# Late up products of three feed-forward layers as [feature, token], with the high and low activations side by side

## The chip, the cores and the metric

The kernel runs on one core of one Trainium2 chip. The metric is the device time of one execution in microseconds. TensorE (PE in the rows) multiplies: a stationary 128 x 128 operand is loaded (PEld), and a moving operand of up to 512 columns streams past it into PSUM. VectorE (DVE), ScalarE (ACT) and GpSimd (POOL) do the rest, and SyncE (SP) issues the DMAs of the weights. Each engine works through its own queue in order and waits for semaphores of the others.

## The reference, cut to what matters

Two transformer blocks run one after the other over 256 tokens of width 1024, each with two layers. Only the feed-forward parts and the norms behind them matter here:

```python
def first_block(x, ...):                      # RMS norms, x + ...
    for l in range(DEPTH):                    # DEPTH = 2
        ...                                   # two attentions, gates, w_out
        h2 = rms_norm(x, mlp_norm_g[l])
        x = x + jnp.square(jax.nn.relu(h2 @ w_up[l])) @ w_down[l]        # 1024 -> 4096 -> 1024

def _swiglu(x, w1, w3, w2):                   # 1024 -> 2816 -> 1024
    return (jax.nn.silu(x @ w1) * (x @ w3)) @ w2

def second_block(x, mem, ...):
    a = DEEPNORM_ALPHA
    for l in range(DEPTH):
        x = _layer_norm(a * x + 0.5 * _swiglu(x, ffn1_w1[l], ffn1_w3[l], ffn1_w2[l]), ...)
        mix = _token_mixing(x, w_in[l], ...)  # four branches, ends with @ w_o
        x = _layer_norm(a * x + mix, ...)
        x = _layer_norm(a * x + _cross_attention(x, mem, ...), ...)
        x = _layer_norm(a * x + 0.5 * _swiglu(x, ffn2_w1[l], ffn2_w3[l], ffn2_w2[l]), ...)
```

All of it is in float32.

## The kernel before, in words

**Numbers.** A float32 operand is held as two tiles, the high part (a rounded copy in the type fp32r, made by ScalarE) and the low part (what the rounding left, subtracted by VectorE). A product of two operands is three products per 128-deep K tile: high x high, high x low weights, low x high weights, all added in PSUM. `mm_a` (L423) issues them with a 128-token half of the activations as the stationary operand and up to 512 columns of weights moving, so that the result is [token, feature]. The 256 tokens are two halves, m = 0 and 1; the residual rows of the halves are the tiles x0 and x1.

**Weights.** They arrive in the order of use as units of 512 KB (128 partitions x 1024 numbers, here two K tiles x 512 columns). SyncE issues their DMAs into the pool `raw` of 7 buffers, ScalarE casts the high part (L325) and VectorE subtracts the low part (L318); these two are called a conversion here. Conversions run about five units ahead of the use (`LOOK`), and not more than 11 (`WIDE`) or 9 (`NARROW`) units past the oldest one that is held. High and low parts, the activations `xt` of a stage and others share the pool `b4` of 27 buffers.

**A feed-forward stage** is `ffn` (L695). The stage's activations stand in `xt`, eight K tiles x 256 tokens, high and low apart. `up` (L702) makes the products of one chunk of 512 features (in swiglu the last chunk has 256) for both halves, per matrix; `act_relu2` or `act_swiglu` makes h of them, still [token, feature]. The down product needs features on partitions, so `trans` (L729) transposes h on TensorE, four 128 x 128 blocks per half and chunk (L419), and splits the result into high and low (L570, L571, or L573, L574 with a scale). `dn` (L750) is the down product: six 512-column products per half, output half of D and unit. The first chunks (two in w_up, one in each swiglu matrix) go through `gemm_first` (L492), which begins with half 0 while half 1 is still being normalized.

**The end of a stage** is `leave` (L536), used by `ffn` and by `gemm_out` (the projections w_out, w_o and that of the cross attention). It runs the last three units of a down or output product for half 0, then for half 1, with the chains `update` (L639) of the halves beside them. A chain is, on VectorE: for each half of D, x updated from PSUM (L646 or L648) and its statistics (L652); then the aggregate (L657), x less its mean times the gain (L670), the reciprocal root in eight small steps (L589 to L596), and x times that plus the bias (L672). Then `transposed` (L681) turns x0, later x1, on TensorE into the next stage's `xt` and splits it (L570, L571). The last layer norm of the program writes the output instead.

**What sets the order.** A list scheduler orders the instructions of every engine when the program is built, by dependencies, priorities and its own estimate of durations. The chains have a high priority (`hasten`, L370); conversions have none. On the chip the order of each engine's queue is fixed.

## Time and profile before

| | us |
|---|---|
| median of 3 runs | 2226.20 |
| lowest and highest | 2226.19, 2227.69 |
| the profiled execution | 2228.81 |
| its span in the profile | 2227.0 |
| TensorE busy | 2187.6 (98%) |
| VectorE busy | 1520.3 (68%) |
| ScalarE busy | 1078.1 (48%) |
| GpSimd busy | 118.7 (5%) |

The mean granted clock of TensorE in the profiled execution is 0.997 of full. In the rows, a line such as L413 is a line of the kernel before; `mm` (L413) issues every product and `tr` (L419) every transpose, so shapes and tile names tell the work apart. The mean of one matmul that a group prints is longer than its share of the busy time, since matmuls overlap in the pipeline; busy time divided by the count is what one adds to the stream. Of a row with brackets the bracket is the idle time before it and what ended that.

### The profile page before, as it was taken

The numbers are of one execution on the slowest core, as the hardware profiler recorded it, in microseconds if no ns is written. First come the engines' busy times: TensorE is split into PE (matmuls) and PEld (weight loads), VectorE is DVE, ScalarE is ACT, GpSimd is POOL, SyncE is SP. The second block draws the span as 40 slices with busy tenths as digits, with TensorE's granted clock in tenths as the row PEclk, the third lists the DMA queues.
The fourth block names the chain that finished last, engine by engine and source line by source line (L and its number), as shares of the span: only waits on it lengthen the run. The fifth ranks groups of instructions, "written<-read, shape, count | busy, mean of one in ns | idle before, by whom it ended". The sixth has DMA issues, their size and how long they took to land. (4 is left out here: it accounts for less than half of the span.)

```text
span 2227.0 us, 30615 instructions
## 1 busy us (share of the span) xinstructions
PE 2187.6 (98%) x11454; PEld 1852.9 (83%) x11454; DVE 1520.3 (68%) x2456; ACT 1078.1 (48%) x1681; POOL 118.7 (5%) x191
## 2 busy tenths in 40 slices
PE   7999999999999999999999999999999999999998
PEld 6878888878888888889888888888888988897886
DVE  7677457768545555888878765575578887777555
ACT  5664444583434444466654444444345665444442
POOL 2000001000000000013000000000000310000000
PEclk9999999999999999999999999999999999999999
DMA  7355465445555555454556455555645554754561
GB/s 272 117 168 193 167 221 168 152 144 185 172 207 176 184 208 203 162 181 151 171 182 206 157 185 208 208 167 192 229 153 184 170 152 152 235 181 151 181 244 48
DMA packets 114709, 399.91 MB, mean 180 GB/s; under 512 B 13056, under 2 KB 13728, under 8 KB 114560
## 3 DMA queue, kind: packets, MB, share of 16 engines
q1 hardware_dynamic: 107712, 374.30, 49.4%
q0 software_dynamic: 6848, 23.66, 3.2%
q8 instruction: 90, 1.47, 0.3%
q14 instruction: 59, 0.48, 0.1%
HBM read 396.85 MB, written 1.05 MB: 179 GB/s over the span
## 5 line engine op out<-in xcount | busy, mean ns | idle before, releaser
L413 PE MATMUL ps<-b,b 128*128 128x512 f32 (+7 forms) x10412 | 2090.1, 363 | 5.4 <-DVE b L571 2.5
L413 PEld LDWEIGHTS ps<-b,b 128*128 128x128 f32 (+2 forms) x10412 | 1736.8, 188 | 316.3 <-issue 11.3
L318 DVE TENSOR_TENSOR b<-raw,b 128x1024 fp32r<-128x1024 f32 (+3 forms) x738 | 844.6, 1181 | 50.5 <-PE ps L413 28.9
L325 ACT CAST b<-raw 128x1024 fp32r<-128x1024 f32 (+3 forms) x738 | 717.3, 1019 | 197.5 <-PE ps L413 138.8
L570 ACT CAST b<-ps 128x512 fp32r<-128x512 f32 (+2 forms) x188 | 100.8, 571 | 394.6 <-PE ps L419 313.7
L571 DVE TENSOR_TENSOR b<-ps,b 128x512 fp32r<-128x512 f32 (+2 forms) x188 | 118.7, 663 | 194.8 <-ACT b L570 194.4
L574 DVE SCALAR_TENSOR_TENSOR b<-ps,b 128x512 fp32r<-128x512 f32 (+1 forms) x64 | 39.1, 653 | 257.5 <-ACT b L573 257.5
L573 ACT ACTIVATE b<-ps 128x512 fp32r<-128x512 f32 (+1 forms) x64 | 33.1, 569 | 342.8 <-PE ps L419 342.8
L419 PE MATMUL ps<-cst,b 128*128 128x128 f32 (+1 forms) x810 | 106.6, 274 | 13.3 <-DVE b L667 11.6
L419 PEld LDWEIGHTS ps<-cst,b 128*128 128x128 f32 (+1 forms) x810 | 93.8, 140 | 25.3 <-DVE b L667 11.8
L601 POOL DMA_DIRECT2D b<-in_rows_dram x55 | 29.7, 543 | 1363.5 <-PE ps L413 743.6
L1544 ACT ACTIVATE b<-b,sm 128x128 f32<-128x128 f32 (+1 forms) x128 | 56.6, 447 | 7.9 <-DVE sm L819 7.8
L786 DVE TENSOR_TENSOR b<-b,ps 128x512 f32<-128x512 f32 (+1 forms) x48 | 30.8, 642 | 38.6 <-PE ps L413 37.3
L879 DVE TENSOR_TENSOR b<-ps,b 128x512 f32<-128x512 f32 x32 | 22.1, 689 | 27.1 <-PE ps L413 27.0
L881 ACT ACTIVATE b<-b 128x512 f32<-128x512 f32 x32 | 20.0, 630 | 41.8 <-DVE b L879 41.8
L652 DVE BATCH_NORM_STATS2 sm<-x 128x6 f32<-128x512 f32 x48 | 32.8, 688 | 3.9 <-DMA x<-in_x_dram 3.6
L1564 DVE TENSOR_TENSOR b<-b,sm 128x512 f32<-128x512 f32 x48 | 34.2, 740 | 0.3
L775 ACT ACTIVATE b<-ps 128x512 f32<-128x512 f32 x32 | 19.3, 603 | 28.4 <-PE ps L413 28.4
L784 ACT ACTIVATE b<-ps 128x512 f32<-128x512 f32 (+1 forms) x48 | 27.0, 562 | 12.0 <-issue 7.3
L785 DVE SCALAR_TENSOR_TENSOR b<-b,ps 128x512 f32<-128x512 f32 (+1 forms) x48 | 30.7, 639 | 0.0
L776 DVE SCALAR_TENSOR_TENSOR b<-ps,b 128x512 f32<-128x512 f32 x32 | 21.8, 688 | 12.6 <-ACT b L775 12.6
L419 PE MATMUL ps<-cst,x 128*128 128x128 f32 x128 | 19.5, 286 | 10.5 <-DVE x L672 10.4
(170 smaller groups left out, 753.5 us busy)
## 6 DMA issues: line engine op xcount, KB each, us to landing
raw<-in_ffn_w_dram SPq DMA_DIRECT2D x248, 512.0 KB, 5.7
raw<-in_w_in_dram SPq DMA_DIRECT2D x184, 512.0 KB, 4.6
raw<-in_w_up_dram SPq DMA_DIRECT2D x64, 512.0 KB, 5.0
raw<-in_w_down_dram SPq DMA_DIRECT2D x64, 512.0 KB, 4.9
b<-in_rows_dram POOLq DMA_DIRECT2D x19, 512.0 KB, 7.0
raw<-in_w_out_dram SPq DMA_DIRECT2D x16, 512.0 KB, 4.4
raw<-in_ffn_w_dram SPq DMA_DIRECT2D x32, 256.0 KB, 2.9
raw<-in_w_o_dram SPq DMA_DIRECT2D x16, 512.0 KB, 5.7
```

What stands on the lines that cost most here:

```text
L318: self.nc.vector.tensor_sub(lo[:, :n], r[:, :n], hi[:, :n].bitcast(F32))
L325: self.nc.scalar.copy(hi[:, :n], r[:, :n])
L413: i = self.nc.tensor.matmul(out, lhsT, rhs, start=start, stop=stop, skip_group_check=True)
L419: i = self.nc.tensor.transpose(out, in_, self.ident[:k, :k])
L570: nc.scalar.copy(hi, src)
L571: nc.vector.tensor_sub(lo, src, hi.bitcast(F32))
L573: nc.scalar.activation(hi, src, AF.Copy, scale=scale)
L574: nc.vector.scalar_tensor_tensor(lo, src, scale, hi.bitcast(F32), op0=ALU.mult, op1=ALU.subtract)
L652: nc.vector.bn_stats(st[:, 6 * i:6 * i + 6], x[:, c])
L786: nc.vector.tensor_mul(h[:, :w], r[:, :w], pss[1])
L1544: nc.scalar.activation(p[:, i], p[:, i], AF.Exp, scale=-1.0, bias=nm[:, at + i:at + i + 1], accum_out=den[:, at + i:at + i + 1])
L1564: e.tensor_mul(p, p, rinv[:, at:at + n].unsqueeze(2).broadcast_to((P, n, w)))
```

## The change

From a stage's third chunk on (w_up) or the second (each swiglu matrix), the up products take 256 features at a time. The weights are now the stationary operand and the activations move: high and low activations stand side by side in one constant tile (`StageXT`, 8 K tiles x 2 x 256), so the high weights see 512 columns (high and low activations at once) and the low weights 256. The result is [feature, token], with the products of the low activations in a PSUM half of their own; ScalarE copies that half out and VectorE adds the other to it. `late_relu2` and `late_swiglu` work on the sum, and the split writes the operand of the down product directly, without transposes, into the pool `b2`. A unit of these chunks holds four K tiles x 256 columns. The pool `b4` loses four buffers, those that the stage's `xt` used. `leave` takes the last three units as before.

```diff
+FIRST_UPS = {"w_up": 2, "ffn1_w1_2": 1, "ffn1_w3_2": 1, "ffn2_w1_2": 1, "ffn2_w3_2": 1}
+def _ups(name, n):
+    m = 512 * FIRST_UPS[name]
+    return _even(m) + [[(i, i + 256)] for i in range(m, n, 256)]
...
-    "w_up": (D, _even(FF1)),
+    "w_up": (D, _ups("w_up", FF1)),
...
+def _deep(name, c):
+    return 4 if c >= FIRST_UPS.get(name, 99) else 2
...
     def open(self, ctx):
...
-        for tag, bufs in (("raw", RAW), ("b4", B4 - RAW), ("b2", B2), ("b1", B1), ("h", 8), ("sm", 24)):
+        for tag, bufs in (("raw", RAW), ("b4", B4 - RAW - 4), ("b2", B2), ("b1", B1), ("h", 8), ("sm", 24)):
...
+        self.xt_tile = self.const.tile([P, 8, 2, S], F32R, name="xt")
...
     def leave(self, name, l, us, product, acc, a, kind):
...
-        self.xt = self.new_xt()
+        self.xt = StageXT(self.xt_tile)
...
-    def ffn(self, l, ups, down, act, scale, a, kind):
+    def ffn(self, l, ups, down, act, late_act, scale, a, kind):
...
-        def up(c, between):
-            pss = [[], []]
-            for i, name in enumerate(ups):
-                nu, cw = self.dims(name, c)
-                ps = [self.ps(), self.ps()]
-                for u in range(nu):
-                    unit = self.get(name, l, c, u)
-                    for m in range(2):
-                        self.mm_a(ps[m][:, :cw], xt, m, unit, cw, 2 * u, 2, u == 0, u == nu - 1)
...
+        def up(c, between=None):
+            both = []
+            for i, name in enumerate(ups):
+                ps = [self.ps() for _ in range(2)]
+                for u in range(2):
+                    unit = self.get(name, l, c, u)
+                    for f in range(2):
+                        for k in range(4):
+                            o = k * 256 + f * P
+                            first, last = u == 0 and k == 0, u == 1 and k == 3
+                            self.mm(ps[f], unit[0][:, o:o + P], xt.both(4 * u + k), first, False)
+                            self.mm(ps[f][:, :S], unit[1][:, o:o + P], xt.get(4 * u + k)[0], False, last)
+                        if u == 1:
+                            if f == 0:
+                                both.append(self.t("b2", [P, 2, S]))
+                            s = both[-1][:, f]
+                            nc.scalar.copy(s, ps[f][:, S:])
+                            nc.vector.tensor_add(s, ps[f][:, :S], s)
...
+            h = late_act(both)
+            t = XT(self, 2, "b2")
+            hi, lo = t.pair(0)
+            self.split(hi, lo, h, scale)
+            ht[2 * ahead + c - ahead] = t, 0
...
+        up_first(range(ahead))
+        todo = deque(range(us - 3))
         if ahead == 2:
-            trans(seq[0])
-            dn([0, 1])
-        for i in range(ahead, n):
...
+            trans(0)
+            dn(todo.popleft())
+            dn(todo.popleft())
+        n = len(WEIGHTS[ups[0]][1])
+        for c in range(ahead, n):
+            if c == n - 1:
+                kind = kind()
+            up(c, (lambda: trans(ahead - 1)) if c == ahead else None)
+            if c != n - 2:
+                dn(todo.popleft())
+        while todo:
+            dn(todo.popleft())
+        self.leave(down, l, range(us - 3, us), product, acc, a, kind)
...
+    def late_relu2(self, both):
+        h = self.t("b2", [P, 2, S])
+        self.nc.vector.scalar_tensor_tensor(h, both[0], 0.0, both[0], op0=ALU.max, op1=ALU.mult)
+        return h
+    def late_swiglu(self, both):
+        nc, (a, b) = self.nc, both
+        r = self.t("b2", [P, 2, S])
+        nc.scalar.activation(r, a, AF.Tanh, scale=0.5)
+        nc.vector.scalar_tensor_tensor(r, r, 1.0, a, op0=ALU.add, op1=ALU.mult)
+        nc.vector.tensor_mul(r, r, b)
+        return r
...
+class StageXT:
...
+    def get(self, k, m=None):
+        c = slice(0, S) if m is None else slice(m * P, m * P + P)
+        return self.t[:, k, 0, c], self.t[:, k, 1, c]
+    def both(self, k):
+        return self.t[:, k].rearrange("p h t -> p (h t)")
```

The line numbers move: L318, L413, L419 are L335, L430, L436 in the changed kernel; the chain's L648, L657, L670, L672 are L666, L675, L688, L690, and the root's L589 to L596 are L607 to L614. The new copy and addition are L763 and L764.

In the order of the built program, TensorE in the late chunks of w_up, layer 0 of block 1. A row names the result in PSUM, then the moving and the stationary operand. Before: products of a chunk (`b_489`, `b_490` are weights, high and low, `b_373`, `b_374` activations), then transposes of the chunk ahead, then the chunk's next unit:

```order
L413 MATMUL ps_2357<-b_489_2284,b_373_1746 128x512
L413 MATMUL ps_2357<-b_490_2285,b_373_1746 128x512
L413 MATMUL ps_2357<-b_489_2284,b_374_1747 128x512 x2
L419 MATMUL ps_2396<-cst,b_486_2277 128x128 x4
L419 MATMUL ps_2403<-cst,b_488_2281 128x128 x4
L413 MATMUL ps_2356<-b_492_2302,b_375_1748 128x512
L413 MATMUL ps_2356<-b_493_2303,b_375_1748 128x512
```

After, in such a chunk, where `b_514` and `b_519` are high, `b_515` and `b_520` low weight tiles:

```order
L430 MATMUL ps_2568<-xt,b_514_2456 128x512
L430 MATMUL ps_2568<-xt,b_515_2457 128x256
L430 MATMUL ps_2568<-xt,b_514_2456 128x512
L430 MATMUL ps_2568<-xt,b_515_2457 128x256
L430 MATMUL ps_2567<-xt,b_519_2476 128x512
L430 MATMUL ps_2567<-xt,b_520_2477 128x256
```

The eight transposes between the products are gone, and products of 512 and 256 columns alternate.

VectorE at the end of ffn1 in layer 0 of block 2, before: the chain of x0 from the aggregate to its last step (x0 and x1 are the halves' rows, sm small tiles, ps PSUM):

```order
L657 BN_AGGR sm_1656_7881<-sm_1655_7880 128x2
L670 SCALAR_TENSOR_TENSOR x0_82<-x0_82,sm_1656_7881,b4_1591_7604 128x512 x2
L589 TENSOR_SCALAR sm_1663_7917<-sm_1656_7881 128x1
L590 TENSOR_SCALAR sm_1664_7918<-sm_1663_7917 128x1
L584 SCALAR_TENSOR_TENSOR sm_1665_7919<-sm_1664_7918,sm_1663_7917 128x1
L592 SCALAR_TENSOR_TENSOR sm_1665_7919<-sm_1665_7919 128x1
L593 SCALAR_TENSOR_TENSOR sm_1664_7918<-sm_1665_7919,sm_1664_7918 128x1
L584 SCALAR_TENSOR_TENSOR sm_1665_7919<-sm_1664_7918,sm_1663_7917 128x1
L595 SCALAR_TENSOR_TENSOR sm_1664_7918<-sm_1665_7919,sm_1664_7918 128x1
L596 TENSOR_SCALAR sm_1664_7918<-sm_1664_7918 128x1
L672 SCALAR_TENSOR_TENSOR x0_82<-x0_82,sm_1664_7918,b4_1592_7606 128x512 x2
L648 SCALAR_TENSOR_TENSOR x1_83<-x1_83,ps_1441_6843 128x512
```

After, the same place from the aggregate on; x0's last step (L690) follows six rows below the last one shown, with one more conversion among them:

```order
L675 BN_AGGR sm_1665_8174<-sm_1664_8173 128x2
L688 SCALAR_TENSOR_TENSOR x0_83<-x0_83,sm_1665_8174,b4_1623_7981 128x512 x2
L607 TENSOR_SCALAR sm_1672_8210<-sm_1665_8174 128x1
L335 TENSOR_TENSOR b4_1676_8232<-raw_1654_8135,b4_1675_8231 128x1024
L608 TENSOR_SCALAR sm_1673_8211<-sm_1672_8210 128x1
L335 TENSOR_TENSOR b4_1688_8293<-raw_1659_8151,b4_1687_8292 128x1024
L602 SCALAR_TENSOR_TENSOR sm_1674_8212<-sm_1673_8211,sm_1672_8210 128x1
L335 TENSOR_TENSOR b4_1695_8318<-raw_1660_8153,b4_1694_8317 128x1024
L610 SCALAR_TENSOR_TENSOR sm_1674_8212<-sm_1674_8212 128x1
L335 TENSOR_TENSOR b4_1698_8332<-raw_1663_8165,b4_1697_8331 128x1024
L666 SCALAR_TENSOR_TENSOR x1_84<-x1_84,ps_1439_6988 128x512
L611 SCALAR_TENSOR_TENSOR sm_1673_8211<-sm_1674_8212,sm_1673_8211 128x1
```

Conversions and an update of x1 moved between the small steps of x0's chain.

TensorE at the same place, before, where `ps_1446` gathers the last down product of half 1 and the transposes are those of x0:

```order
L413 MATMUL ps_1446_6863<-b4_1632_7800,b4_1636_7819 128x512 x2
L413 MATMUL ps_1446_6863<-b4_1643_7838,b4_1635_7818 128x512
L419 MATMUL ps_1671_7972<-cst_81,x0_82 128x128 x4
L413 MATMUL ps_1446_6863<-b4_1644_7839,b4_1635_7818 128x512
L419 MATMUL ps_1672_7979<-cst_81,x0_82 128x128 x4
L413 MATMUL ps_1446_6863<-b4_1643_7838,b4_1635_7818 128x512
L413 MATMUL ps_1446_6863<-b4_1644_7839,b4_1635_7818 128x512
L413 MATMUL ps_1446_6863<-b4_1643_7838,b4_1636_7819 128x512 x2
```

After, with `ps_1439` in the same part:

```order
L430 MATMUL ps_1439_6988<-b4_1652_8131,b2_1644_8091 128x512
L430 MATMUL ps_1439_6988<-b4_1653_8132,b2_1644_8091 128x512
L430 MATMUL ps_1439_6988<-b4_1652_8131,b2_1645_8092 128x512 x2
L436 MATMUL ps_1680_8265<-cst_82,x0_83 128x128 x4
L436 MATMUL ps_1681_8272<-cst_82,x0_83 128x128 x4
L430 MATMUL ps_1690_8298<-b4_1655_8143,xt_79 128x440
```

The last five products of half 1 stand ahead of x0's transposes, and the next product behind these is the first of the next stage.

## Rows read from the trace of the kernel before

**Rows 1.** Page, part 1: busy us (share of the span) and instructions.

```profile
PE 2187.6 (98%) x11454; PEld 1852.9 (83%) x11454; DVE 1520.3 (68%) x2456; ACT 1078.1 (48%) x1681; POOL 118.7 (5%) x191
```

**Rows 2.** Waits on PE: line, waited for: us in total, times, longest.

```profile
PE ps L419 <- DVE x L672: 10.4, 9, 2.5
```

**Rows 3.** Groups by shape on PE: count, then busy us, mean ns, idle before.

```profile
L413 PE MATMUL ps<-b,b 128*128 128x512 f32 x7344 | 1708.2, 392 | 3.7 <-ACT b L570 1.1 <-DVE b L571 1.0 <-DVE b L318 1.0
L413 PE MATMUL ps<-b,b 128*128 128x256 f32 x2296 | 291.5, 286 | 1.5 <-DVE b L571 1.5
L419 PE MATMUL ps<-cst,b 128*128 128x128 f32 x776 | 102.4, 275 | 13.3 <-DVE b L667 11.6 <-ACT b L570 0.8 <-DVE b L629 0.5
```

**Rows 4.** Groups by shape on PE from 740 to 900 us, in ffn1.

```profile
L413 PE MATMUL ps<-b,b 128*128 128x512 f32 x634 | 145.5, 390 | 0.0
L413 PE MATMUL ps<-b,b 128*128 128x256 f32 x96 | 11.9, 284 | 0.0
```

**Rows 5.** Timeline of PE, 300 to 332 us: start, us, instruction [wait].

```profile
318.52 1.03 PE L419 MATMUL ps<-cst,b 128*128 128x128 f32 x8
319.31 12.95 PE L413 MATMUL ps<-b,b 128*128 128x512 f32 x56
```

**Rows 6.** Windows, ffn1: PE, PEld, DVE, ACT, POOL busy; PEclk, DMA share, GB/s.

```profile
735.00:905.00 170.00, 170.00 (x819) 143.26 (x818) 92.46 (x103) 71.89 (x87) 1.06 (x2) 1.00 0.54 198
```

**Rows 7.** Groups by shape: an addition from PSUM and a copy out of it.

```profile
L1673 DVE TENSOR_TENSOR b<-ps,b 64x256 f32<-64x256 f32 x48 | 18.7, 418 | 6.8 <-ACT b L1672 6.2
L1672 ACT COPY b<-ps 64x256 f32<-64x256 f32 x48 | 16.7, 366 | 3.3 <-PE ps L413 1.2 <-DVE b L1673 0.8
```

**Rows 8.** Timeline, 895 to 935 us: end of ffn1 in layer 0, into mixing.

```profile
903.61 0.68 DVE L648 SCALAR_TENSOR_TENSOR x<-x,ps 128x512 f32<-128x512 f32 x1
...
907.84 0.14 DVE L589 TENSOR_SCALAR sm<-sm 128x1 f32<-128x1 f32 x1
908.02 0.15 DVE L590 TENSOR_SCALAR sm<-sm 128x1 int32<-128x1 int32 x1
...
910.56 0.66 PE L419 MATMUL ps<-cst,x 128*128 128x128 f32 x4 [0.58 <-DVE x L672]
...
918.53 0.15 DVE L589 TENSOR_SCALAR sm<-sm 128x1 f32<-128x1 f32 x1
918.59 1.22 DVE L318 TENSOR_TENSOR b<-raw,b 128x1024 fp32r<-128x1024 f32 x1
919.72 0.15 DVE L590 TENSOR_SCALAR sm<-sm 128x1 int32<-128x1 int32 x1
...
924.63 1.32 PE L419 MATMUL ps<-cst,x 128*128 128x128 f32 x8 [1.60 <-DVE x L672]
```

**Rows 9.** Timeline: ends of w_o, xattn, ffn2 in layer 0, two of layer 1.

```profile
1220.38 0.63 PE L419 MATMUL ps<-cst,x 128*128 128x128 f32 x4 [0.24 <-DVE x L672]
...
1222.87 1.28 DVE L652 BATCH_NORM_STATS2 sm<-x 128x6 f32<-128x512 f32 x2
...
1279.80 1.38 PE L419 MATMUL ps<-cst,x 128*128 128x128 f32 x8 [2.53 <-DVE x L672]
...
1467.94 1.29 PE L419 MATMUL ps<-cst,x 128*128 128x128 f32 x8
...
1671.48 1.32 PE L419 MATMUL ps<-cst,x 128*128 128x128 f32 x8 [1.60 <-DVE x L672]
...
2028.22 1.79 PE L419 MATMUL ps<-cst,x 128*128 128x128 f32 x8 [2.52 <-DVE x L672]
```

**Rows 10.** Windows behind four waits of TensorE; PEclk is the third number from the end.

```profile
1281.00:1285.00 4.00, 4.00 (x12) 3.09 (x12) 3.95 (x8) 3.47 (x5) 0.00 (x0) 0.59 0.00 0
1672.00:1677.00 5.00, 4.98 (x19) 4.07 (x18) 3.57 (x9) 1.79 (x3) 0.00 (x0) 0.66 0.60 206
2028.00:2032.00 4.00, 3.78 (x14) 3.06 (x15) 3.61 (x8) 2.54 (x4) 0.00 (x0) 0.57 0.00 0
925.00:930.00 5.00, 4.98 (x27) 4.16 (x26) 4.77 (x11) 2.42 (x4) 0.00 (x0) 1.00 0.65 209
```

More of the change, by code (lines that the diff above doesn't have):

```diff
@@ L117, in _units @@
         for c, ch in enumerate(chunks):
-            for u in range((k // P + 1) // 2):
-                nk = min(2, k // P - 2 * u)
+            d = _deep(name, c)
+            for u in range((k // P + d - 1) // d):
+                nk = min(d, k // P - d * u)
                 out[(l, c, u)] = (off, nk, _width(ch))
@@ L134, in _pack @@
         at = 0
+        first = _deep(name, c) * u * P
         for a, b in chunks[c]:
-            blk = w[l, 2 * u * P:(2 * u + nk) * P, a:b].reshape(nk, P, b - a)
+            blk = w[l, first:first + nk * P, a:b].reshape(nk, P, b - a)
             dst[:, :, at:at + b - a] = blk.transpose(1, 0, 2)
@@ L481, in dims @@
         k, chunks = WEIGHTS[name]
-        return (k // P + 1) // 2, _width(chunks[c])
+        d = _deep(name, c)
+        return (k // P + d - 1) // d, _width(chunks[c])
     def nk(self, name, u):
@@ L692, in into_xt @@
             yield
-    def ffn(self, l, ups, down, act, scale, a, kind):
-        hid = WEIGHTS[down][0]
-        n = (hid + 511) // 512
+    def ffn(self, l, ups, down, act, late_act, scale, a, kind):
+        nc = self.nc
+        us = WEIGHTS[down][0] // 256
         xt = self.xt
+        ahead = FIRST_UPS[ups[0]]
         acc = [[None, None], [None, None]]
         hs, ht = {}, {}
-        def up(c, between):
-            pss = [[], []]
-            for i, name in enumerate(ups):
-                nu, cw = self.dims(name, c)
-                ps = [self.ps(), self.ps()]
-                for u in range(nu):
-                    unit = self.get(name, l, c, u)
-                    for m in range(2):
-                        self.mm_a(ps[m][:, :cw], xt, m, unit, cw, 2 * u, 2, u == 0, u == nu - 1)
-                    if i == 0 and u == nu // 2 - 1:
-                        between()
-                for m in range(2):
-                    pss[m].append(ps[m][:, :cw])
-            for m in range(2):
-                hs[c, m] = act(pss[m], cw)
         def up_first(cs):
@@ L729, in trans @@
         def trans(c):
-            ht[c] = self.new_xt(4)
+            t = self.new_xt(4)
             for m in range(2):
-                h, w = hs.pop((c, m))
+                h, _ = hs.pop((c, m))
                 ps = self.ps()
-                k = w // P
-                for i in range(k):
+                for i in range(4):
                     self.tr(ps[:, i * P:i * P + P], h[:, i * P:i * P + P])
-                hi, lo = ht[c].block(0, m, k)
-                self.split(hi, lo, ps[:, :w].rearrange("p (k t) -> p k t", k=k), scale)
-        nus = [(min(512, hid - 512 * c) + 255) // 256 for c in range(n)]
-        seq = [c for c in range(n) if nus[c] == 2]
-        seq[1:1] = [c for c in range(n) if nus[c] == 1]
-        first_u, last_u = 0, 2 * seq[-1] + 1
+                hi, lo = t.block(0, m)
+                self.split(hi, lo, ps.rearrange("p (k t) -> p k t", k=4), scale)
+            ht[2 * c] = t, 0
+            ht[2 * c + 1] = t, 2
+        def up(c, between=None):
[16 more added lines that the diff above has]
+                            nc.vector.tensor_add(s, ps[f][:, :S], s)
+                    if i == 0 and u == 0 and between is not None:
+                        between()
+            h = late_act(both)
[3 more added lines that the diff above has]
+            ht[2 * ahead + c - ahead] = t, 0
         def product(m, cc, u, unit):
@@ L747, in product, with dn @@
                 acc[m][cc] = self.ps()
[L748 to L769 removed]
+            t, k = ht[u]
+            self.mm_a(acc[m][cc], t, m, unit, 512, k, 2, u == 0, u == us - 1)
+        def dn(u):
+            for cc in range(2):
+                unit = self.get(down, l, cc, u)
+                for m in range(2):
+                    product(m, cc, u, unit)
+        up_first(range(ahead))
+        todo = deque(range(us - 3))
+        if ahead == 2:
+            trans(0)
[4 more added lines that the diff above has]
+            if c == n - 1:
+                kind = kind()
+            up(c, (lambda: trans(ahead - 1)) if c == ahead else None)
[4 more added lines that the diff above has]
+        self.leave(down, l, range(us - 3, us), product, acc, a, kind)
     def act_relu2(self, pss, w):
@@ L1029, in swiglu @@
         self.nu = WIDE
[L1030 removed]
+        self.ffn(l, [f"{which}_w1_2", f"{which}_w3_2"], f"{which}_w2_2", self.act_swiglu, self.late_swiglu, 0.25, ALPHA, kind)
     def block2(self, l):
@@ L1456, in pair, with __init__, block @@
         return hi[:, k:k + 2], lo[:, k:k + 2]
+class StageXT:
+    def __init__(self, t):
+        self.t = t
+    def get(self, k, m=None):
[3 more added lines that the diff above has]
+        return self.t[:, k].rearrange("p h t -> p (h t)")
+    def block(self, k, m, n=4):
+        c = slice(m * P, m * P + P)
+        return self.t[:, k:k + n, 0, c], self.t[:, k:k + n, 1, c]
 class Group:
```

28 lines of the change are left out of this document (6 added, 22 removed).

## The prediction

> **What bounds the kernel now.** I read the busy table of the page first. TensorE is busy 98% of the span, VectorE 68%, ScalarE 48% [rows 1]; with one core and a TensorE that hardly rests, the time is the sum of TensorE's instructions plus its waits plus what a lowered clock costs. So the change has two accounts: what it does to the number and length of TensorE's instructions, and what it does to TensorE's few waits. The second view is the table of waits on TensorE: the entry that belongs to stages the change touches is 10.4 us in 9 waits for L672, the last step of a layer norm [rows 2]. These are the ends of the stages of block 2: the normed half x0 or x1 must be finished on VectorE before TensorE can transpose it. Nothing in the feed-forward stage itself holds TensorE up: between 735 and 905 us it is busy 170.00 of 170 us, with VectorE at 92.46 and ScalarE at 71.89 [rows 6]. So what the change gains must come from TensorE's own instructions in the feed-forward stages, and what it may lose must come at the layer norms, where VectorE is on the path.
>
> **Part 1: instructions of TensorE.** Per 512 late features and K tile, six products of 512 columns become four of 512 and four of 256: the same 3072 columns, two more instructions. Over the program (3072 late features in two layers of w_up, 2304 in eight swiglu matrices, whose last 256 features were already 256 columns wide) that takes away 576 products of 512 columns and adds 1152 of 256. The groups by shape give 1708.2/7344 = 232.6 ns for 512 columns and 291.5/2296 = 127.0 ns for 256 [rows 3] (busy over count; the mean printed beside it counts overlap twice). So -576 x 0.2326 = -134.0 us and +1152 x 0.1270 = +146.3 us: **+12.3 us**. In the stretch 740 to 900 the same division gives 229.5 and 124.0 ns [rows 4], and so +10.7 us.
>
> The transposes of the activations go: 24 late chunk halves of 512 columns in w_up (96 transposes) and 144 in swiglu, 240 in all. By group 102.4/776 = 132 ns each [rows 3]: **-31.7 us**. The other end is the distance of starts: eight of them at 318.52, the next product at 319.31, so 99 ns each [rows 5], which gives -23.8 us. I take the group's figure, since it is what a long stream is worth: net **-19.4 us**; the ends are -13.1 (99 ns, stretch prices) and -21.0 (132 ns, stretch prices).
>
> The surplus of 12.3 us is a fixed part of each instruction, some 21 ns beyond half of a 512-column product here. The Trainium skill, in TensorE: Matmul & The Clock Gate, section Back-to-back issue gap, gives an isolated gap of N/2.4 + 2.5 ns for N columns at the full clock; by that the exchange would cost only about 1.4 us (an estimate by that page) and the sum would be 11 us lower. The stream here shows 232.6 ns where the rule gives 215.8, so the rows decide.
>
> **Part 2: VectorE and ScalarE in the feed-forward stages.** Each chunk of 256 features and matrix now ends with two ScalarE copies out of PSUM and two VectorE additions, 128x256. The nearest rows are a copy and an addition from PSUM of 64x256: 366 and 418 ns [rows 7]. A swiglu has 9 chunks x 2 matrices x 2 = 36 of each: at most 15 us more on VectorE and 13 on ScalarE, before the splits that are saved. 92.46 + 15 and 71.89 + 13 of 170 us leave a third of VectorE free, and TensorE has a group of down products between one chunk's evacuation and the need for its result. I price this at nothing; if the cover fails it is rival 4. The weight DMAs of the last chunks become fewer and larger, and SP issues them several units ahead of their use: nothing. The one shared tile of stage activations can be written only when the stage before has read it; its readers stand whole groups of down products earlier: nothing.
>
> **Part 3: where VectorE's conversions stand.** This is the part that the diff does not tell. The scheduler placed VectorE's weight conversions (L318, 1.2 us each) anew. I counted in the order those that stand in x0's chain, from x0's second update to its last step, at the seven layer-norm ends that follow a matrix product and lead into another stage: end of ffn1 1 before, 6 now (both layers); of w_o 2 and 8 (both); of xattn 1 and 7 (both); of ffn2 in layer 0 1 and 6. That is **39 more**. At five of these ends (all but xattn, which had it) x1's second update and its statistics also come into x0's chain. The pieces of order above show the first end.
>
> What one costs is seen in x1's chain at this same end before. Without a conversion between them L589 and L590 start at 907.84 and 908.02, 0.18 us apart; with one they start at 918.53 and 919.72, 1.19 us apart [rows 8]. So an inserted conversion of 1.22 us lengthens the chain by **1.01 us**, a little less than its duration. x1's update (0.68 [rows 8]) and statistics (1.28/2 = 0.64 [rows 9]) by the same share add 1.1 us. Longer chains: ffn1 5 x 1.01 + 1.1 = 6.2; w_o 6 x 1.01 + 1.1 = 7.2; xattn 6 x 1.01 = 6.1; ffn2 5 x 1.01 + 1.1 = 6.2.
>
> What covers it? Before, TensorE already waits for x0 at three of the four kinds of end: 0.58 at ffn1, 0.24 at w_o, 2.53 at xattn; at ffn2 it does not wait [rows 8, 9]. So there is no slack, and the chain's growth goes into the wait, less the products that are now ahead of the transposes instead of behind them: five at ffn1 and w_o (5 x 0.23 = 1.2 us), and about as much at ffn2 with its unknown slack. Growth of the waits: 5.0 twice, 6.0 twice, 6.1 twice, 5.0 once: **+39.2 us**.
>
> On the other side x1's chain loses its conversions (four to six of them), and TensorE has its 24 first products of the next stage and more in front of x1's transposes as before. Of the 10.4 us waited for L672 [rows 2], x0's are 2 x (0.58 + 0.24 + 2.53) = 6.7, if the second layer is as the first; the other 3.7, such as the 1.60 at 924.63 [rows 8], may go: **-3.7 us**. The ends of block 1 (rms) keep their order.
>
> **Part 4: the clock after a wait.** After the 2.53 us wait the granted clock from 1281 to 1285 is 0.59 of full, that is largely the 1.2 GHz level, and TensorE was idle for part of the six us ahead of it; 4 x 0.41 = 1.6 us are lost. After a wait of 1.60 us it is 0.66 from 1672 to 1677 (1.7 us), after one of 2.52 us 0.57 from 2028 to 2032 (1.7 us). After the 1.60 us wait at 924 it stays at 1.00 [rows 8 to 10]. Three of four waits of this length cost about 1.7 us, 5.0 in all. With seven longer waits, at the same three in four: 7 x 0.75 x 1.7 = 8.9, so **+3.9 us**.
>
> **Sum.** -19.4 + 39.2 - 3.7 + 3.9 = **+20.0 us**. Against the profiled execution of 2228.8 that is 2248.8; the median of the runs stands 2.6 us below the profiled one, so I forecast 2226.2 + 20.0 = **2246.2 us**, slower by 0.9%. A difference of about 0.2% (4.5 us) is what a measurement of this kernel can tell from none.
>
> **Rivals.**
> 1. *Only TensorE's account counts.* If VectorE stood so far ahead of TensorE at the stage ends that its conversions were done before x0's second product ends, the chain would not lengthen and 2226.2 - 19.4 = 2206.8 would result: faster. For it: VectorE is busy only 68%. Against it: its queue is in order, the conversions stand behind x0's second update, which needs TensorE's last product of x0, and before x0's chain TensorE already waits. It decides if the x0 waits stay below 2.8 us each (19.4/7). Chance 0.06.
> 2. *The clock.* If the low level lasted as long as the wait before it, seven waits of 5.6, 6.2, 8.6 (twice each) and 5.0, 45.8 us in all, would cost half of it, 22.9 us, where I put 8.9: 2260. For it: three waits of 1.6 to 2.5 us were each followed by 1.6 to 1.7 lost. Against it: at 924 nothing followed. The Trainium skill (the same page, section HAM oscillation — how this bites in real kernels) has idle stretches of TensorE followed by a throttled one; by that the loss would come after each of the seven, and the trace agrees at three of four. Chance 0.08.
> 3. *The two accounts cancel.* If the conversions cost about half (0.5 us) because they fill gaps of the chain's dependent small steps, +39.2 becomes about +20 and the time stays at 2226. Against it: the 1.19 against 0.18 in rows 8. Chance 0.04.
> 4. *The evacuation holds TensorE.* If at each of the 60 late chunks (24 in w_up, 36 in swiglu) TensorE waited 0.5 us for copy and addition before its PSUM is free, 30 us would come on top: 2276. Against it: the free third of VectorE and the down products in between. Chance 0.04.
>
> That the change doesn't do what it says is excluded by the order of the built program: the transposes are gone and the 256-column products are there.
>
> **How the numbers follow.** The forecast has 0.78. Its own ends: with the larger gain (-21.0), conversions at 0.85 us (39 x 0.16 = 6 less) and no change of the clock, +8: 2234; with the smaller gain (-13.1), conversions at 1.16 and x1's waits kept, +36: 2262, which takes in rival 2. Range 2234 to 2262; outside are rivals 1, 3 and 4 with 0.14. Faster 0.07, same 0.04, slower 0.89.
>
> **What the changed profile would show.** Part 1: some 11790 matmuls, 256-column products at 124 to 127 ns and TensorE still without a wait in the feed-forward stages; a wait for the new L763 or L764 there would mean rival 4. Part 3: the waits for x0's last step (L690) at the seven ends of 5 to 9 us, 46 us in all, with conversions (L335) between the small steps in the timeline of VectorE. Waits of 1 to 3 us there would make the prediction wrong towards rival 1. Part 4: clock at 0.5 to 0.7 for 3 to 5 us behind most of these waits; if for as long as the wait, rival 2.

## The result and the profile after

The changed kernel takes **2265.45 us** (median of 4 runs, 2264.35 to 2265.97) against 2226.94 us for the kernel before in the same job (4 runs): ratio 1.0167, 95% interval 1.0155 to 1.0179, or 38.5 us slower. The forecast was 20.0 us slower, with a range up to 2262. The direction and the mechanisms were right; two terms of the sum, the gain of TensorE's own instructions and the price of the clock, were mis-sized by 17 us together. The profiled execution took 2265.97 us, its span is 2264.2, 37.2 more than before.

The page's busy table (answers to [rows 1]):

```profile
PE 2189.5 (97%) x11790; PEld 1865.9 (82%) x11790; DVE 1623.8 (72%) x2620; ACT 1154.2 (51%) x1825; POOL 116.0 (5%) x191
```

336 more matmuls (576 products more, 240 transposes fewer), and TensorE's busy time is nearly what it was: what its own instructions gained, a lower clock took back, as is read below. In the feed-forward stage nothing holds it, as before [rows 6]; the window of ffn1, same columns:

```profile
730.00:900.00 170.00, 170.00 (x882) 144.74 (x881) 110.19 (x135) 85.32 (x118) 1.06 (x2) 1.00 0.58 187
```

170.00 of 170 us busy; VectorE rose from 92.46 to 110.19 and ScalarE from 71.89 to 85.32 (the prediction had 107 and 85). So the copies and additions are hidden, and rival 4 is out.

The time is lost at the stage ends. Waits of TensorE (answers to [rows 2]), then the timeline of its x0 transposes at four of the seven ends (ffn1, w_o, xattn, ffn2 of layer 0; answers to [rows 8, 9]):

```profile
PE ps L436 <- DVE x L690: 45.2, 7, 8.6
```

```profile
909.36 1.94 PE L436 MATMUL ps<-cst,x 128*128 128x128 f32 x8 [4.80 <-DVE x L690]
...
1225.19 1.94 PE L436 MATMUL ps<-cst,x 128*128 128x128 f32 x8 [6.82 <-DVE x L690]
...
1292.25 1.94 PE L436 MATMUL ps<-cst,x 128*128 128x128 f32 x8 [8.60 <-DVE x L690]
...
1486.68 1.94 PE L436 MATMUL ps<-cst,x 128*128 128x128 f32 x8 [4.80 <-DVE x L690]
```

Seven waits, 45.2 us, where the prediction put 45.8; all are x0's, x1's are gone. That is 34.8 us more than the 10.4 of before. All idle time of TensorE, span less busy time, rose from 39.4 to 74.7 us, so by 35.3: these waits are nearly all of it. Eight transposes now take 1.94 us instead of the 1.38 that eight take behind a short wait at the full clock (e5_fill below): the clock is down. VectorE at the first of these ends shows why x0 is late (timeline, 900 to 909 us):

```profile
900.57 0.15 DVE L607 TENSOR_SCALAR sm<-sm 128x1 f32<-128x1 f32 x1
900.63 1.22 DVE L335 TENSOR_TENSOR b<-raw,b 128x1024 fp32r<-128x1024 f32 x1
901.77 0.15 DVE L608 TENSOR_SCALAR sm<-sm 128x1 int32<-128x1 int32 x1
901.83 1.22 DVE L335 TENSOR_TENSOR b<-raw,b 128x1024 fp32r<-128x1024 f32 x1
902.96 0.22 DVE L602 SCALAR_TENSOR_TENSOR sm<-sm,sm 128x1 f32<-128x1 f32 x1
903.09 1.22 DVE L335 TENSOR_TENSOR b<-raw,b 128x1024 fp32r<-128x1024 f32 x1
...
905.43 0.68 DVE L666 SCALAR_TENSOR_TENSOR x<-x,ps 128x512 f32<-128x512 f32 x1
...
908.46 1.42 DVE L690 SCALAR_TENSOR_TENSOR x<-x,sm,b 128x512 f32<-128x512 f32 x2
```

From the first small step at 900.57 to x0's last step at 908.46 are 7.9 us; before it was 907.84 to 909.75, 1.9 us. Each conversion that stands between two small steps pushes the next one by 1.2 us. These conversions are of 1024 columns: they belong to the second group of weights of the next stage, whose products begin only behind x0's transposes and the first 24 products; the last of the 880-column ones, which come first, started at 888.28.

The clock behind the seven waits (windows, columns as in [rows 10]):

```profile
909.00:912.00 3.00, 2.64 (x10) 2.40 (x11) 2.93 (x7) 1.17 (x2) 0.00 (x0) 0.52 0.32 130
1225.00:1230.00 5.00, 4.81 (x23) 4.84 (x24) 4.90 (x11) 1.17 (x2) 0.00 (x0) 0.50 0.59 210
1292.00:1298.00 6.00, 5.75 (x17) 4.71 (x18) 5.76 (x15) 2.22 (x3) 0.00 (x0) 0.50 0.35 139
1486.00:1493.00 7.00, 6.32 (x19) 5.18 (x20) 6.65 (x18) 2.21 (x3) 0.00 (x0) 0.51 0.37 147
1681.00:1687.00 6.00, 5.82 (x19) 5.27 (x20) 5.72 (x16) 2.22 (x3) 0.00 (x0) 0.50 0.15 60
1999.00:2005.00 6.00, 5.62 (x27) 5.65 (x28) 5.76 (x15) 1.18 (x2) 0.00 (x0) 0.52 0.47 172
2066.00:2070.00 4.00, 3.31 (x12) 2.87 (x13) 3.93 (x8) 1.17 (x2) 0.00 (x0) 0.54 0.67 246
```

Behind each of the seven, TensorE runs at the 1.2 GHz level for 3 to 7 us. Length times what is missing to 1, as the prediction counted it: 1.4 + 2.5 + 3.0 + 3.4 + 3.0 + 2.9 + 1.8 = 18.0 us, against 5.0 before. That count is too high: it takes in idle time, up to 0.7 us in a window, and it takes every instruction to be twice as long at half the clock, which the eight transposes above are not (1.94 us against 1.38). Two runs below keep the clock up and allow a direct comparison. From x0's transposes to the first product behind x1's, the same instructions take **13.3 us** less in e5_fill than here, summed over the seven ends. TensorE is busy for 4.1 us less in e7_before_behind, where no wait is followed by a low clock, than in the kernel before (2183.5 against 2187.6). So the clock costs about 9 us more than before, not 13.

The span's 37.2 us are then 35.3 of waits and 9.2 of clock, less some **7 us** that TensorE's own instructions got shorter. That rest can be compared with the stream itself. TensorE in ffn1 after (timeline; a group of `ps<-xt,b` holds 512- and 256-column products in turn, and is printed by the shape of its first):

```profile
753.78 5.64 PE L430 MATMUL ps<-b,b 128*128 128x512 f32 x24
759.26 11.45 PE L430 MATMUL ps<-xt,b 128*128 128x512 f32 x64
770.55 5.67 PE L430 MATMUL ps<-b,b 128*128 128x512 f32 x24
```

64 late up products take 770.55 - 759.26 = 11.29 us, 352.8 ns a pair; 24 down products 5.48 us, 228.3 ns each. 1536 pairs are 541.9 us; the 2112 products of 512 columns that they replace, at 228.3, and the 384 of 256 at the 124.0 of [rows 4] are 529.8. That is +12.1 us, as forecast (+12.3). The transposes were worth 240 x 99 ns = 23.8 us [rows 5], not the 31.7 I took: net -11.7. The span leaves 7, so the pieces overstate the gain by 4 to 5 us. Some 1.6 of them come with the constant tile alone (TensorE busy 2183.5 us in e7_before_behind, 2185.1 in e8_xt_behind, which adds the tile and the smaller pool); the other 3 are not placed.

### The profile page after: what moved, and what is told of

Read it like the earlier page. It is cut to its first block, busy times and chain, and to the rows that moved or that the text cites. A ratio compares the mean times of both kernels' runs of the same rounds, so it can differ in the third digit from the quotient of the medians.

```text
span 2264.2 us, 31445 instructions
## 1 busy us (share of the span) xinstructions
PE 2189.5 (97%) x11790; PEld 1865.9 (82%) x11790; DVE 1623.8 (72%) x2620; ACT 1154.2 (51%) x1825; POOL 116.0 (5%) x191
## 4 chain that ended last, share of the span: by engine, by line
PE 85%; DVE 7%; issue 5%; ACT 2%; DMA 1%; POOL 0%; SPq 0%; DVEq 0%; ACTq 0%; POOLq 0%
PE ps L430 82%; PE ps L436 3%; DVE b L335 2%; DVE sm L670 1%; DVE x L666 1%; DVE b L589 0%; ACT b L342 0%; DMA b<-in_mem_dram 0%; DMA raw<-in_w_in_dram 0%; DVE x L688 0%; ACT b L588 0%; ACT b L1555 0%; ACT b L1607 0%; DVE x L690 0%; DVE xt L589 0%
## 5 line engine op out<-in xcount | busy, mean ns | idle before, releaser
L335 DVE TENSOR_TENSOR b<-raw,b 128x1024 fp32r<-128x1024 f32 (+3 forms) x722 | 859.2, 1204 | 225.8 <-PE ps L430 198.7
L430 PE MATMUL ps<-b,b 128*128 128x512 f32 (+7 forms) x4076 | 846.8, 369 | 2.6 <-DVE b L589 1.5
L430 PEld LDWEIGHTS ps<-b,b 128*128 128x128 f32 (+3 forms) x4076 | 677.0, 185 | 140.9 <-issue 10.0
L430 PE MATMUL ps<-xt,b 128*128 128x512 f32 (+1 forms) x4416 | 716.9, 322 | 0.0
L430 PEld LDWEIGHTS ps<-xt,b 128*128 128x128 f32 x4416 | 636.8, 189 | 72.9
L430 PE MATMUL ps<-b,xt 128*128 128x512 f32 (+2 forms) x2496 | 568.9, 386 | 1.9 <-DVE b L335 1.0
L430 PEld LDWEIGHTS ps<-b,xt 128*128 128x128 f32 x2496 | 459.3, 191 | 96.5 <-ACT xt L588 3.4
L588 ACT CAST b<-ps 128x512 fp32r<-128x512 f32 (+3 forms) x116 | 61.1, 560 | 150.7 <-PE ps L430 78.9
L589 DVE TENSOR_TENSOR b<-ps,b 128x512 fp32r<-128x512 f32 (+3 forms) x116 | 71.9, 649 | 78.7 <-ACT b L588 78.4
L764 DVE TENSOR_TENSOR b<-ps,b 128x256 f32<-128x256 f32 x192 | 81.0, 424 | 49.4 <-ACT b L763 46.7
L763 ACT COPY b<-ps 128x256 f32<-128x256 f32 x192 | 70.9, 369 | 49.5 <-PE ps L430 49.3
L436 PE MATMUL ps<-cst,b 128*128 128x128 f32 (+1 forms) x570 | 75.4, 275 | 14.7 <-DVE b L685 11.8
L436 PEld LDWEIGHTS ps<-cst,b 128*128 128x128 f32 (+1 forms) x570 | 65.6, 141 | 23.1 <-DVE b L685 12.0
L436 PE MATMUL ps<-cst,x 128*128 128x128 f32 x128 | 22.9, 339 | 45.2 <-DVE x L690 45.2
L436 PEld LDWEIGHTS ps<-cst,x 128*128 128x128 f32 x128 | 19.4, 177 | 48.9 <-issue 48.0
L666 DVE SCALAR_TENSOR_TENSOR x<-x,ps 128x512 f32<-128x512 f32 x32 | 21.9, 685 | 33.0 <-PE ps L430 32.7
```

Source lines behind the costliest of these rows:

```text
L335: self.nc.vector.tensor_sub(lo[:, :n], r[:, :n], hi[:, :n].bitcast(F32))
L430: i = self.nc.tensor.matmul(out, lhsT, rhs, start=start, stop=stop, skip_group_check=True)
L436: i = self.nc.tensor.transpose(out, in_, self.ident[:k, :k])
L588: nc.scalar.copy(hi, src)
L589: nc.vector.tensor_sub(lo, src, hi.bitcast(F32))
L666: ins = nc.vector.scalar_tensor_tensor(x[:, c], x[:, c], a, acc[i], op0=ALU.mult, op1=ALU.add)
```

## The experiments

Theory A: the stage activations' move into a tile of their own lets the conversions come early, the scheduler sets them into x0's chain, the chain makes the waits and the waits the low clock. Theory B: the late chunks give VectorE so much work that it falls behind at the stage ends, wherever the conversions stand. All times are medians, beside the kernel before in the same job.

| kernel | us | before | ratio, 95% interval |
|---|---|---|---|
| e1_behind | 2216.73 | 2228.22 | 0.9949, 0.9935 to 0.9964 |
| e2_xt_only | 2274.74 | 2228.22 | 1.0209, 1.0192 to 1.0226 |
| e3_grouped | 2259.10 | 2228.22 | 1.0144, 1.0129 to 1.0159 |
| e4_twice | 2257.74 | 2228.22 | 1.0132, 1.0117 to 1.0147 |
| e5_fill | 2247.44 | 2228.25 | 1.0088, 1.0074 to 1.0102 |
| e6_behind_grouped | 2211.50 | 2228.25 | 0.9927, 0.9915 to 0.9940 |
| e7_before_behind | 2221.47 | 2228.25 | 0.9970, 0.9959 to 0.9982 |
| e9_pool_only | 2234.89 | 2228.25 | 1.0031, 1.0020 to 1.0042 |
| e8_xt_behind | 2227.96 | 2228.47 | 0.9998, 0.9989 to 1.0007 |

### The conversions behind the chains (e1_behind)

```diff
     def _lo(self):
...
-            self.nc.vector.tensor_sub(lo[:, :n], r[:, :n], hi[:, :n].bitcast(F32))
+            ins = self.nc.vector.tensor_sub(lo[:, :n], r[:, :n], hi[:, :n].bitcast(F32))
+            self.subs.append((j, ins))
...
     def leave(self, name, l, us, product, acc, a, kind):
...
+        end = self.pos + 2 * len(us) if self.order is not None else 0
...
     def arrive(self):
         self.settle()
+            for j, ins in self.subs:
+                if j >= end + 5:
+                    self.after(ins, self.done)
+                elif j >= end + 3:
+                    self.after(ins, done0)
         self.transposed(1)
```

Here `j` numbers the units, `end` is the first unit of the next stage, `done0` the last step of x0 and `self.done`, by then, that of x1.

> The changed kernel with one edit: at the seven layer-norm ends the conversions of units past the next stage's third wait for x0's last step, those past its fifth for x1's. No work is left out. In the built order the conversions in x0's chain fall from 6, 8, 7, 6 per end to 0, 3, 0, 0. Theory A (the place of the conversions makes the waits, and the waits the low clock): the 45 us of waits for L690 fall to 5 to 12 us, the low-clock stretches mostly vanish (11 of the 17 us lost in them come back), and the time falls from 2265 to 2215 to 2228. Theory B (VectorE simply has too much work at the stage ends since the late chunks gave it more, and the conversions have to be made there anyway): the waits turn up again as waits of the first products for L335, and the time stays above 2250.

2216.73 us: 48.7 below the changed kernel and 0.5% below the kernel before. Waits of TensorE, the entries for the layer norms (L707 is L690 here, L606 the split into xt, L338 the conversions):

```profile
PE ps L434 <- DVE xt L606: 4.2, 6, 1.7
PE ps L440 <- DVE x L707: 3.6, 7, 0.6
PE ps L434 <- DVE b L338: 1.9, 3, 0.6
```

VectorE's small steps at the end of ffn1 in layer 0 stand together again, TensorE's transposes come with no wait, and the window behind them has the full clock:

```profile
900.49 0.15 DVE L624 TENSOR_SCALAR sm<-sm 128x1 f32<-128x1 f32 x1
900.67 0.15 DVE L625 TENSOR_SCALAR sm<-sm 128x1 int32<-128x1 int32 x1
...
902.14 1.42 DVE L707 SCALAR_TENSOR_TENSOR x<-x,sm,b 128x512 f32<-128x512 f32 x2
```

```profile
904.07 1.04 PE L440 MATMUL ps<-cst,x 128*128 128x128 f32 x8
```

```profile
904.00:910.00 6.00, 5.89 (x32) 4.92 (x30) 5.96 (x10) 2.02 (x3) 0.00 (x0) 1.00 0.47 146
```

Waits for L690 fall from 45.2 to 3.6 us, only 1.9 us turn up for conversions and 4.2 for the split. VectorE has the same work as in the changed kernel (2620 instructions); it was the order. TensorE's order changed with it at the end of ffn1 (six products of half 1, 1.4 us, stand behind x0's transposes again), but not at the end of w_o in layer 0, and the wait there fell from 6.82 to 0.57 us all the same. Theory B is out.

### The tile alone (e2_xt_only), and the pool alone (e9_pool_only)

```diff
-        for tag, bufs in (("raw", RAW), ("b4", B4 - RAW), ("b2", B2), ("b1", B1), ("h", 8), ("sm", 24)):
+        for tag, bufs in (("raw", RAW), ("b4", B4 - RAW - 4), ("b2", B2), ("b1", B1), ("h", 8), ("sm", 24)):
...
+        self.xt_tile = self.const.tile([P, 8, 2, S], F32R, name="xt")
...
-        self.xt = self.new_xt()
+        self.xt = StageXT(self.xt_tile)
```

e9_pool_only has the first pair of lines alone.

> The kernel before with the stage activations in one constant tile and the pool four buffers smaller, and nothing else: its feed-forward layers, transposes and all, are as before. In the built order the conversions in x0's chain rise from 1, 2, 1, 1 to 8, 8, 7, 8 per end. Theory A (the tile's move out of the pool is what lets the conversions come early): slower than before by 40 to 55 us, 2267 to 2282, with waits of 5 to 9 us for the last step of x0 at the seven ends and a low clock behind them. Theory B (the extra VectorE work of the late chunks is the cause): none of that work is here, so 2226 within 5 us.

> The kernel before with its pool b4 four buffers smaller, 23 instead of 27, and the stage activations still in it. With e2_xt_only it tells which half of that edit lets the conversions into the chains. In the built order they rise only to 3, 4, 1, 2 in x0's chain, nine more in all. If the smaller pool were the cause of e2_xt_only's 46 us: 2270. If the tile's move out of the pool is: 2224 to 2238.

e2_xt_only takes 2274.74 us, 46.5 more than the kernel before, with its feed-forward layers untouched. Its waits (L673 is x0's last step):

```profile
PE ps L420 <- DVE x L673: 47.2, 7, 7.5
```

47.2 us in 7 waits, and a mean clock of 0.987 as in the changed kernel. e9_pool_only takes 2234.89, 6.6 more. So the smaller pool by itself makes a seventh of it, and the rest comes only with the tile's move out of the rotating pool; no run moves the tile and leaves the pool as it was. The changed kernel's whole loss is in this part, which the feed-forward products only need as a layout: from e2_xt_only to the changed kernel the time falls by 9.3 us. Why the scheduler lets the conversions come earlier once the activations no longer take buffers of the pool in turn, I can only argue (a conversion's buffers come free with others' last use); no run shows why.

### The clock (e5_fill)

```diff
-                if m == 1 and i == len(todo) - 2 and (kind is None or kind[0] != "last"):
+                if m == 1 and i == len(todo) - 1 and (kind is None or kind[0] != "last"):
+                    if self.order is not None and kind is not None and kind[0] == 'ln':
+                        self.fills, self.warm = {'w_o_2': 24, 'xattn_wo_2': 32}.get(name, 15), units[c, u][0]
                     self.transposed(0)
...
             ps = self.ps()
+            for _ in range(self.fills if b == 0 else 0):
+                self.mm(ps, self.warm[:, :P], self.warm[:, :512], True, True)
```

> The changed kernel with products that nobody reads put behind the last down or output product of a stage: 15 at the feed-forward ends, 24 at w_o, 32 at xattn, so that TensorE works (3.4, 5.4 and 7.3 us) while it waits for x0; x0's transposes stand behind them. In the built order one conversion fewer stands in each of the seven chains (5, 7, 6, 5), which alone is worth 7 us. Theory A, its second half (idle TensorE brings the low clock, and the low clock behind the waits costs 17 us in the changed kernel): the low stretches behind the seven waits go, and the time is 2265 - 7 - 15 = 2243. Rival (the low clock comes from something else at the stage ends, such as VectorE's load): it stays, 2258.

2247.44 us, 18.0 below the changed kernel, where 22 was expected, 15 for the clock and 7 for one conversion fewer in each chain. TensorE at the end of xattn in layer 0, first the fill products, then x0's transposes; and two windows there:

```profile
1280.95 7.42 PE L430 MATMUL ps<-b 128*128 128x512 f32 x32
1288.60 1.38 PE L436 MATMUL ps<-cst,x 128*128 128x128 f32 x8 [0.24 <-DVE x L693]
1289.94 8.46 PE L430 MATMUL ps<-b,xt 128*128 128x512 f32 x36
1298.23 1.03 PE L436 MATMUL ps<-cst,x 128*128 128x128 f32 x8
1299.02 14.15 PE L430 MATMUL ps<-b,xt 128*128 128x512 f32 x60
```

```profile
1286.00:1290.00 4.00, 3.66 (x20) 2.53 (x18) 3.86 (x8) 0.59 (x1) 0.00 (x0) 1.00 0.94 313
1290.00:1294.00 4.00, 4.00 (x18) 3.31 (x19) 3.96 (x8) 0.59 (x1) 0.00 (x0) 1.00 0.54 170
```

The same place in the changed kernel, from the transposes at 1292.25 on, and the window ahead of them:

```profile
1294.02 10.45 PE L430 MATMUL ps<-b,xt 128*128 128x512 f32 x36
1304.30 1.03 PE L436 MATMUL ps<-cst,x 128*128 128x128 f32 x8
1305.09 14.15 PE L430 MATMUL ps<-b,xt 128*128 128x512 f32 x60
```

```profile
1288.00:1292.00 4.00, 0.00 (x0) 0.00 (x0) 3.89 (x9) 0.00 (x0) 0.00 (x0) 0.50 0.89 302
```

The clock stays at 1.00 where it was 0.50, though VectorE is as busy as in the changed kernel (3.86 and 3.96 of 4 us against 3.89): idle TensorE brought it down. The same 52 instructions take 10.42 us from 1288.60 to 1299.02, where they took 12.84. The other six ends give 1.06, 1.85, 2.48, 2.43, 2.12 and 0.96 us in the same way, 13.3 in all. So some 13 of the 18 us are the clock's and some 5 those of the shorter chains, not 15 and 7. Keeping TensorE busy with waste gets a third of what the order gets.

### What the transposes and the products cost (e4_twice, e3_grouped)

e4_twice doubles the line of `trans` that issues a transpose. e3_grouped is:

```diff
                         for k in range(4):
                             o = k * 256 + f * P
-                            first, last = u == 0 and k == 0, u == 1 and k == 3
-                            self.mm(ps[f], unit[0][:, o:o + P], xt.both(4 * u + k), first, False)
-                            self.mm(ps[f][:, :S], unit[1][:, o:o + P], xt.get(4 * u + k)[0], False, last)
+                            self.mm(ps[f], unit[0][:, o:o + P], xt.both(4 * u + k), u == 0 and k == 0, False)
+                        for k in range(4):
+                            o = k * 256 + f * P
+                            self.mm(ps[f][:, :S], unit[1][:, o:o + P], xt.get(4 * u + k)[0], False, u == 1 and k == 3)
```

> The kernel before with each transpose of the activations h in the feed-forward stages made twice into the same place, 304 more in all; nothing else. It prices the operation that the change removes. By the distance of starts (99 ns) 304 cost 30 us: 2256. By busy time over count (132 ns), as the prediction took it, 40 us: 2266. If the stream hides them: 2226 to 2235.

> The changed kernel, in which each late block of four K tiles takes its four 512-column products first and then its four 256-column ones, instead of alternating; the sums are the same. In the trace of the changed kernel a start after a 512-column product comes 236 ns later when a 256-column one follows, and 227 ns when a 512 follows; after a 256 it is 117 ns (512 follows) or 120 (256 follows). Theory C (the alternation costs the stream these 9 ns): 384 groups of four save 3 x 9 - 3 x 3 = 18 ns each, 6.9 us, 2258 instead of 2265. Rival (what follows does not matter, the 236 ns come with the 512 column moving operand in the one tile xt): 2265 within 2, and 236 ns also between two 512-column products.

e4_twice: 29.5 us for 304 transposes, 97 ns each. The place of [rows 5] with sixteen instead of eight (timeline of TensorE):

```profile
322.12 1.91 PE L419 MATMUL ps<-cst,b 128*128 128x128 f32 x16
323.78 16.38 PE L413 MATMUL ps<-b,b 128*128 128x512 f32 x71
```

1.66 us to the next product where it was 0.79: 109 ns for each added one, 99 for each of a whole group that goes. Both are far from 132.

e3_grouped: 2259.10, 6.4 us below the changed kernel (6.9 expected). The same stretch of ffn1 as above:

```profile
757.65 11.36 PE L430 MATMUL ps<-xt,b 128*128 128x512 f32 x64
768.85 5.65 PE L430 MATMUL ps<-b,b 128*128 128x512 f32 x24
```

11.20 us for the 64 products instead of 11.29. Over 48 such stretches that is 4.3 us, the most part of the 6.4. e6_behind_grouped against e1_behind, where the clock stays up in both, gives 5.2. It is a small cost of alternating, but a real one.

### The feed-forward change by itself (e7_before_behind, e8_xt_behind, e6_behind_grouped)

e7_before_behind is the kernel before with the edit of e1_behind; e8_xt_behind is e2_xt_only with it; e6_behind_grouped has e1_behind's and e3_grouped's edits.

> The kernel before with the edit of e1_behind alone: conversions past the next stage's third unit behind x0's last step, past its fifth behind x1's. It tells how much of e1_behind's gain is the order's and how much the feed-forward change's. Theory: TensorE's own instructions are some 7 to 9 us shorter with the change, so with the same guarded ends the kernel before stands at 2224 to 2226, about where it was, if its x1 waits (4 us) and low clock (5 us) are all that the guard can give it: 2217 to 2226. Rival (the feed-forward change is worth nothing by itself, e1_behind's gain is all the guard's): 2216, equal to e1_behind.

> e2_xt_only with the edit of e1_behind: the feed-forward layers of the kernel before, the activations in the one constant tile, the smaller pool, and the conversions held behind the chains. Against e1_behind (2216.7) it differs by the feed-forward change alone, with ends that hardly wait in both. If the feed-forward change is worth 9 us, as the traces of before and after add up (240 transposes at 99 ns each, 23.8, less 14 for the products): 2226. If it is worth the 19.4 us of the prediction: 2236. If nothing: 2217.

> The edits of e1_behind and e3_grouped together. They touch different stretches, so the gains should add: 2216.7 - 6.5 = 2210, 0.8% below the kernel before. If the grouping delays the evacuation of a chunk, less: 2213 to 2217.

e8_xt_behind takes 2227.96, e1_behind 2216.73; they differ by the feed-forward change alone, and hardly wait at the ends (in e8_xt_behind 4.8 us for x0's and x1's last steps):

```profile
PE ps L418 <- DVE xt L589: 5.5, 9, 1.6
PE ps L424 <- DVE x L690: 4.8, 8, 0.7
PE ps L418 <- DVE b L322: 3.5, 5, 1.4
```

So the change of the products is worth **11.2 us** here, of which the waits above differ by some 4 (13.8 against 9.7). That leaves some 7 for TensorE's own instructions, less than the 11.7 of the pieces above; the 19.4 of the prediction is out. TensorE's busy times say the same, first e8_xt_behind and e1_behind, then e2_xt_only (the changed kernel's row stands above):

```profile
PE 2185.1 (98%) x11454; PEld 1847.8 (83%) x11454; DVE 1522.7 (68%) x2456; ACT 1080.9 (49%) x1681; POOL 118.9 (5%) x191
PE 2177.6 (98%) x11790; PEld 1853.0 (84%) x11790; DVE 1620.0 (73%) x2620; ACT 1149.7 (52%) x1825; POOL 115.0 (5%) x191
PE 2196.9 (97%) x11454; PEld 1861.3 (82%) x11454; DVE 1525.1 (67%) x2456; ACT 1084.1 (48%) x1681; POOL 118.4 (5%) x191
```

The feed-forward change takes 7.5 us off the first pair and 7.4 off the second (2196.9 to 2189.5). In e1_behind's profiled execution the clock was also low once far from these ends (0.57 from 26 to 30 us), by 1.7 us in the prediction's count, so 7 to 9 us is what can be said. e7_before_behind takes 2221.47: the kernel before gains 6.8 us from guarded ends, so that of e1_behind's 11.5 us against the kernel before 6.8 are the guard's and 4.7 the change's net of its tile. e6_behind_grouped is the fastest, 2211.50, 0.7% below the kernel before and 5.2 us below e1_behind, where 6.5 were expected.

## Why the prediction was wrong

Two terms of the sum failed, both in size: the gain of TensorE's own instructions, -19.4 us forecast and some -7 measured, and the clock, +3.9 forecast and some +9 measured. The waits, +35.5 forecast and +35.3 measured, held.

**What bounds the kernel** held: TensorE's instructions, its few waits and its clock made up the whole difference.

**Part 1, products:** +12.1 us read from one stretch of the stream against +12.3, but too small over the whole program. With the transposes at 97 ns (e4_twice), 23.3 us, a net gain of 7 to 9 leaves 14 to 16 us for the products and whatever goes with them (an estimate from these numbers). The "21 ns beyond half of a 512-column product" is a slip: 127.0 less half of 232.6 is 10.7 ns, and 21 is the whole fixed part by these two prices; the sum does not use it.

**Part 1, transposes:** the term was mis-sized, and this is the largest single miss. I had both ends, 132 ns (busy time over count) and 99 ns (distance of starts), and took the first "since it is what a long stream is worth". They come in groups of eight at most, and the busy time of a group runs on under the next product: at 318.52 eight have 1.03 us of busy time and the next product starts after 0.79 [rows 5]. e4_twice gives 97 ns. 8 us of gain that were never there. The sentence under the profile before, that busy time over the count is what one adds to the stream, is wrong for such short groups.

**Part 2:** right; no wait in the feed-forward stages.

**Part 3:** right in place, mechanism and size: 45.2 us of waits forecast as 45.8 (by kind of end 5.6, 6.2, 8.6 and 5.0 forecast; 4.80, 6.82, 8.60 and 4.80 measured), x1's gone, +34.8 against +35.5. e1_behind shows the mechanism by taking it away.

**Part 4, the clock:** the second mis-sized term: some 9 us measured, 13.0 in the prediction's own count, against 3.9. I priced waits of 5 to 9 us by low stretches behind waits of 1.6 to 2.5 us (1.7 us each, three of four). Behind the longer waits all seven had a low stretch, and by the same count it cost 2.6 us on average (1.9 by the direct comparison). Rival 2 had it at 22.9 in all where 18.0 were read by that count: nearer than the forecast's 8.9. By the direct comparison, 13.3, the forecast is the nearer one, and both are off. The rule of the Trainium skill that I put beside rival 2 (TensorE: Matmul & The Clock Gate, section HAM oscillation — how this bites in real kernels), that idle stretches are followed by a throttled one, is borne out by all seven; e5_fill shows that it is the idling.

**The range:** its upper end put the smaller gain together with the forecast's clock, and rival 2 with the forecast's gain. Both unfavourable ends at once, -13.1 + 39.2 - 3.7 + 17.9, give +40 and 2266. That this is near the 2265.45 measured is luck: the gain was smaller still (7) and the clock cheaper than rival 2 (9 more than before, not 17.9). But the ends of two terms that have nothing to do with each other can fall together, and the range left that out.

**Rivals 1, 3 and 4:** none happened. Rival 1's condition, x0 waits below 2.8 us, is what e1_behind makes true, and its time there (2216.7) is near the 2206.8 it named plus the 12 us by which the gain was overstated.

## What to carry to other kernels

Look at the built order of an engine that is off the critical path when a buffer moves to another pool: here a new layout tile, not the new products, moved 39 conversions into chains that end stages, and cost four times what the products gained (46.5 us in e2_xt_only against 11.2). A few dependencies that hold urgent chains free of work that is not yet needed gave all of it back. When a removed instruction is priced, take the distance from its start to the next start, not busy time over count, and compare the sum of such pieces with the busy time of a whole run; and price idle TensorE at more than the idle time, since the clock falls with it.

## What the hardware showed

- Behind waits of 4.8 to 8.6 us TensorE's clock was at the 1.2 GHz level for 3 to 7 us of work in all seven places, and 1.0 to 2.5 us were lost in each against the same instructions at the full clock. It could be down before TensorE began again: 0.50 from 1288 to 1292 us, with the transposes at 1292.25. Behind a wait of 2.5 us it may fall or not: such a wait at xattn in layer 0 was followed by 0.59 in the kernel before [rows 9, 10] and by 1.00 in e4_twice:

```profile
1296.29 1.29 PE L419 MATMUL ps<-cst,x 128*128 128x128 f32 x8 [2.52 <-DVE x L672]
```

```profile
1297.00:1301.00 4.00, 3.99 (x19) 3.18 (x20) 3.96 (x7) 3.92 (x5) 0.00 (x0) 1.00 0.00 0
```

- Products into a PSUM tile that is overwritten afterwards kept the clock at 1.00 through a wait of 7 us (e5_fill).
- Alternating 512- and 256-column products costs a little more than taking four of each: 11.29 against 11.20 us for 64, and 5.2 us of the whole time between e1_behind and e6_behind_grouped.
